# Softmax on one core: late loads as two tiles of 15 and 13 rows, first load on SyncE, first store held for the third tile

## Chip, cores, metric

One core of a Trainium2 chip. The metric is device time in microseconds (us), the median of several executions of the whole program; "span" is the profiled part of one execution, from its first instruction to its end, and the time is 1.8 us more than the span. All runs quoted here were fast, with a granted clock of 1.0. Ratios are the mean time of one kernel's fast runs over the mean of the other's fast runs of the same rounds, so they are not quite the ratio of the medians quoted beside them. ACT is ScalarE, DVE is VectorE, POOL is GpSimd; SyncE (SP) computes nothing here and issues transfers.

## The reference

```python
x = np.random.randn(16, 1024, 512).astype(np.float32)
x_scaled = x / 2.0
x_max = np.max(x_scaled, axis=-1, keepdims=True)
exp_x = np.exp(x_scaled - x_max)
return exp_x / np.sum(exp_x, axis=-1, keepdims=True)
```

A softmax over 512 columns. The 16384 rows lie as 128 rows on each of 128 partitions; "a row" below means one of these 128, that is 128 x 512 x 4 bytes = 262 KB. 33.55 MB come in and 33.55 MB go out.

## The kernel before

A plan lists the tiles: rows of each chunk, and the place in a buffer of 100 rows. The first eight tiles (3, 7 and six times 15 rows) fill the buffer. The last four go to places that become free; their loads are called late loads. A tile is one transfer; the numbers in its list are its chunks, the rows that DVE and ACT work on at a time.

```python
PLAN = [
    ([3], 0), ([4, 3], 3), ([5] * 3, 10), ([5] * 3, 25), ([5] * 3, 40), ([5] * 3, 55),
    ([5] * 3, 70), ([5] * 3, 85), ([5] * 3, 10), ([4, 3], 3), ([3], 0), ([3], 25),
]
LAG = 2
AFTER = {8: 4, 9: 4, 10: 4, 11: 6}     # late load 8 is issued after tile 4's exponentials, ...
...
# ACT: exponentials; late loads, each behind the stores that free its place
for k, (t, b, c, a) in enumerate(chunks):
    while late and last_chunk[AFTER[late[0]]] < k:
        u = late.pop(0)
        for v in behind[u]:
            nc.scalar.wait_ge(st[v], 16)
        nc.scalar.dma_start(out=sb(u), in_=dram(xf, u)).then_inc(ld[u], 16)
    ...                                # one activation (exp, with its sum) for each row
# DVE: maximum of chunk k, then 1/sum and product of chunk k - 2
for k in range(len(chunks) + LAG):
    if k < len(chunks):
        do_max(k)
    if k >= LAG:
        do_mul(k - LAG)
# SyncE: stores, in order of the tiles
for t in range(len(tiles)):
    nc.sync.wait_ge(s_mul, last_chunk[t] + 1)
    nc.sync.dma_start(out=dram(of, t), in_=sb(t)).then_inc(...)
```

All loads go out on ACT's queue (q10 in the profile), all stores on SyncE's (q1). Tiles are counted from 0, as in the code; the prediction says "the ninth tile" for tile 8.

## Time and profile before

| | before |
|---|---|
| time | 162.19 us (162.18 to 162.22, 4 runs) |
| span of the profiled run | 160.4 us |
| DVE, ACT busy | 132.0 us (82%), 94.5 us (59%) |
| moved | 67.1 MB, 419 GB/s over the span |
| last two loads land | 135.7 and 146.6 us |

The prediction shows the lines of the page, and reads from them that bytes set the time.

### The profile page before, as it was taken

The page shows a single profiled execution, that of the slowest core. Times are in us where ns is not written, and L with a number is a line of the kernel's source. Part 1 is how long each engine was busy: PE and PEld are TensorE (multiplying, and loading weights), DVE is VectorE, ACT ScalarE, POOL GpSimd, SP SyncE. Part 2 cuts the span into 40 slices and gives each one's busy share as a digit, 9 for nine tenths or more (in the row PEclk, how much of TensorE's full clock was granted, in tenths as well). Part 3 has the DMA queues.
Part 4 walks back from the last instruction along what each step waited for, and adds up shares of the span by engine and source line. Part 5 has one row for each costly group of instructions (what it writes and reads, how often), then busy time and mean ns, then how long its engine had stood idle before and what let it go on. Part 6 is the DMA issues. An engine that isn't in the chain of part 4 may idle for free.

```text
span 160.4 us, 480 instructions
## 1 busy us (share of the span) xinstructions
DVE 132.0 (82%) x155; ACT 94.5 (59%) x257; POOL 0.2 (0%) x4
## 2 busy tenths in 40 slices
DVE  0475499999999999999999999999999997704900
ACT  0739076759548646866679666697666875500500
POOL 0000000000000000000000000000000000000000
DMA  7999999999998999999999999998999999999796
GB/s 259 483 402 467 397 426 411 343 464 420 417 483 383 475 391 467 429 429 439 414 460 406 467 391 469 398 467 376 474 432 423 441 429 432 411 448 432 335 408 245
DMA packets 3459, 67.13 MB, mean 419 GB/s; under 512 B 384, under 2 KB 384, under 8 KB 1152
## 3 DMA queue, kind: packets, MB, share of 16 engines
q10 hardware_dynamic: 1728, 33.56, 49.5%
q1 hardware_dynamic: 1728, 33.56, 48.8%
q14 instruction: 3, 0.02, 0.0%
HBM read 33.55 MB, written 33.55 MB: 418 GB/s over the span
## 4 chain that ended last, share of the span: by engine, by line
DVE 49%; DMA 38%; another core or an unknown queue 5%; ACT 1%; issue 0%; DVEq 0%
DMA arena<-in_x_dram 38%; DVE negmax L91 25%; DVE arena L104 13%; DVE arena L111 10%; ACT arena L130 1%; DVE recip L100 1%; DVEq L206 0%
## 5 line engine op out<-in xcount | busy, mean ns | idle before, releaser
L130 ACT ACTIVATE arena<-arena,negmax 128x512 f32<-128x512 f32 x128 | 90.8, 710 | 51.6 <-DVE negmax L91 51.6
L91 DVE TENSOR_REDUCE negmax<-arena 128x5 f32<-128x2560 f32 (+2 forms) x28 | 72.3, 2586 | 19.6 <-DMA arena<-in_x_dram 19.5
L111 DVE TENSOR_SCALAR arena<-arena,recip 128x512 f32<-128x512 f32 x91 | 37.9, 482 | 0.7
L130 ACT ACTIVATION_READ_ACCUMULATOR arena<-arena,negmax 128x1 f32 x128 | 23.9, 187 | 0.0
L104 DVE TENSOR_TENSOR arena<-arena,recip 128x2560 f32<-128x2560 f32 (+2 forms) x8 | 21.0, 2625 | 0.3
L100 DVE RECIPROCAL recip<-sums 128x5 f32<-128x5 f32 (+2 forms) x28 | 4.9, 176 | 0.0
L130 ACT ACT_TABLE_LOAD x1 | 1.3, 1283 | 4.5 <-issue 4.5
L195 POOL MEMSET const-bfloat16-1.0<- 128x1 bf16 x1 | 0.1, 101 | 0.0
L195 POOL MEMSET const-uint8-127<- 128x1 uint8 x1 | 0.1, 101 | 0.0
L195 POOL MEMSET const-float32-0.0<- 128x1 f32 x1 | 0.1, 98 | 0.2 <-issue 0.2
L195 POOL MEMSET const-float32-1.0<- 128x1 f32 x1 | 0.1, 98 | 0.0
## 6 DMA issues: line engine op xcount, KB each, us to landing
arena<-in_x_dram ACTq DMA_DIRECT2D x7, 3840.0 KB, 44.9
out_dram<-arena SPq DMA_DIRECT2D x7, 3840.0 KB, 23.1
arena<-in_x_dram ACTq DMA_DIRECT2D x2, 1792.0 KB, 33.1
out_dram<-arena SPq DMA_DIRECT2D x2, 1792.0 KB, 11.7
arena<-in_x_dram ACTq DMA_DIRECT2D x3, 768.0 KB, 52.2
out_dram<-arena SPq DMA_DIRECT2D x3, 768.0 KB, 6.7
```

The source lines that it names most:

```text
L91: nc.vector.reduce_max(out=negmax[:, b : b + c], in_=arena[:, a : a + c], axis=mybir.AxisListType.X, negate=True,)._wait_ge(ld[t], 16).the ...
L100: nc.vector.reciprocal(out=recip[:, b : b + c], in_=sums[:, b : b + c])._wait_ge(s_exp, k + 1).then_inc(s_rec, 1)
L104: nc.vector.tensor_mul(out=arena[:, a : a + c], in0=arena[:, a : a + c], in1=recip[:, b : b + c].unsqueeze(2).to_broadcast([P, c, D]),)._w ...
L111: ins = nc.vector.tensor_scalar_mul(out=arena[:, a + r], in0=arena[:, a + r], scalar1=recip[:, b + r : b + r + 1],)
L130: ins = nc.scalar.activation(out=arena[:, a + r], in_=arena[:, a + r], func=mybir.ActivationFunctionType.Exp, bias=negmax[:, b + r : b + r ...
L195: nc = _bacc.Bacc("TRN2", target_bir_lowering=False, num_devices=1)
```

## The change

The intent: fewer and larger late transfers, whose packets hold their own against the stores' packets; the first load from an engine that is free; stores kept out of the way of the first loads. At the end, GpSimd's four waits for stores that landed long before are taken out.

```diff
-    ([5] * 3, 70), ([5] * 3, 85), ([5] * 3, 10), ([4, 3], 3), ([3], 0), ([3], 25),
+    ([5] * 3, 70), ([5] * 3, 85), ([5] * 3, 0), ([5, 4, 4], 15),
 ]
+HOLD = 2
-AFTER = {8: 4, 9: 4, 10: 4, 11: 6}
+AFTER = {8: 4, 9: 6}
@@ issue_loads
-            if t not in behind:
+            if t in behind:
+                continue
+            if t == 0:
+                nc.sync.dma_start(out=sb(t), in_=dram(xf, t)).then_inc(ld[t], 16)
+            else:
                 nc.scalar.dma_start(out=sb(t), in_=dram(xf, t)).then_inc(ld[t], 16)
@@ stores
-            nc.sync.wait_ge(s_mul, last_chunk[t] + 1)
+            nc.sync.wait_ge(s_mul, last_chunk[max(t, HOLD)] + 1)
@@ end
-        for t in awaited:
-            nc.gpsimd.wait_ge(st[t], 16)
         nc.gpsimd.wait_ge(s_end, 16 * (len(tiles) - len(awaited)))
```

## The prediction

> **What bounds the kernel now.** I read the page's slices and queues first, then the traffic by stretches, then DVE's and ACT's instructions in order of time, then single DMA issues with their time to landing.
>
> The slices say that the 16 DMA engines are busy from the second slice to the last but one:
>
> ```profile
> DMA  7999999999998999999999999998999999999796
> DMA packets 3459, 67.13 MB, mean 419 GB/s; under 512 B 384, under 2 KB 384, under 8 KB 1152
> ...
> DVE 132.0 (82%) x155; ACT 94.5 (59%) x257; POOL 0.2 (0%) x4
> ```
>
> No compute engine has more than 82%. The traffic by stretches (columns: stretch, its length, busy time of DVE, ACT, POOL, clock, DMA share, GB/s):
>
> ```profile
> 0.00:1.00 1.00, 0.00 (x0) 0.00 (x0) 0.20 (x4) 1.00 0.00 0
> 1.00:2.00 1.00, 0.00 (x0) 0.00 (x0) 0.00 (x0) 1.00 0.85 197
> ...
> 14.00:28.00 14.00, 10.16 (x8) 7.89 (x23) 0.00 (x0) 1.00 0.97 409
> ...
> 111.00:135.00 24.00, 23.27 (x36) 17.86 (x50) 0.00 (x0) 1.00 1.01 433
> 135.00:148.00 13.00, 4.87 (x7) 2.23 (x6) 0.00 (x0) 1.00 1.01 433
> 148.00:150.00 2.00, 1.93 (x7) 1.57 (x5) 0.00 (x0) 1.00 0.71 307
> 150.00:152.00 2.00, 1.97 (x6) 0.66 (x2) 0.00 (x0) 1.00 0.82 344
> ...
> 159.20:160.40 1.20, 0.00 (x0) 0.00 (x0) 0.00 (x0) 1.00 0.00 0
> ```
>
> The full rate is 433 GB/s, and it holds from 135 to 148 us although DVE works only 4.87 of those 13 us. So DVE's waits there cost nothing: bytes set the time. 67.1 MB at 433 GB/s take 155.0 us; the span is 160.4. The other 5.4 us are what a change can touch. From the same answers (length minus MB over 433): 0 to 4 us lose 1.6; 4 to 14 us seem to gain 0.4, because packets are booked by their start; 14 to 28 us lose 0.8; 28 to 148 us lose 0.2 together; 148 to 160.4 us (324 GB/s) lose 3.1. Of these 3.1, 1.0 lies in 148 to 152, 0.9 in 152 to 159.2, 1.2 after the last data.
>
> Why 148 to 152 runs short shows DVE's order:
>
> ```profile
> 137.57 1.68 DVE L111 TENSOR_SCALAR arena<-arena,recip 128x512 f32<-128x512 f32 x4
> 146.65 1.75 DVE L91 TENSOR_REDUCE negmax<-arena 128x3 f32<-128x1536 f32 x1 [7.40 <-DMA arena<-in_x_dram]
> 148.32 0.17 DVE L100 RECIPROCAL recip<-sums 128x3 f32<-128x3 f32 x1
> 148.52 1.28 DVE L111 TENSOR_SCALAR arena<-arena,recip 128x512 f32<-128x512 f32 x3
> ```
>
> The multiply of the tenth tile (148.52) stands in DVE's order behind the maximum of the twelfth, whose load landed at 146.6. Three stores (1.8, 0.8, 0.8 MB) come free only at 149.8 and later, when the ninth tile's store is just running out.
>
> **What the skill says.** "DMA: Bandwidth & Descriptors", section "Where 436 GB/s comes from", gives a ceiling of 435.2 GB/s for the 16 ports. The trace agrees: 433, for reads alone and for stores beside reads. So the change can't raise the rate. The same page, "Queues, rings and completion order": an engine goes round-robin between queues, packet by packet. The trace agrees, with a row of 3 x 2 KB against one of 15 x 2 KB (loads q10, stores q1, from 18 to 27 us: packets, MB):
>
> ```profile
> q10 hardware_dynamic: 109, 3.35, 86.8%
> q1 hardware_dynamic: 109, 0.67, 17.7%
> ```
>
> Equal packets, a fifth of the bytes. From 135 to 140 us it is the other way: 60 load packets have 0.36 MB against 1.60 MB in 52 store packets. So the 3-row late loads were starved by 15-row stores, and took 68.2 and 52.2 us to land. And the page's section "Issuing engines are not separate DMA queues" says that another issuing engine saves issue time alone; the trace of before can't show it.
>
> **The change part by part.**
>
> *First load on SyncE.* ACT's eight issues take 335 to 623 ns each, from 0.13 to 4.4 us. The 7-row load can now be issued about 0.6 us earlier, and both queues feed the engines from 1.3 us on. Of the 1.6 us lost before 4 us I give it 0.2; the first 1.3 us are latency. The two loads now share by packets (6 KB and 14 KB), so the first tile lands after some 20 x 128 KB = 2.6 MB, at about 7.4 us in place of 4.65. That is hidden: DVE stands idle for 3.77 us before the third tile at 18.08 anyway.
>
> *First store waits.* Stores 0, 1 and 2 are all issued when the third tile is multiplied, 44.97 now, 44.7 after (0.3 earlier from the head). Loads run alone until then: 100 rows x 262 KB = 26.2 MB are asked for at the start, and 433 GB/s x 43 us is 18.6 MB, so the engines don't run dry. It saves one change from loads alone to loads beside stores (lost: part of the 0.8 in 14 to 28, and a little after 30 us). I give it 0.2 us.
>
> *Where this comes back.* The ninth tile's load waits on ACT for stores 0, 1 and 2, ahead of the exponentials of chunk 12. Now the third store lands at 44.97 + 21.5 = 66.5, which is just when that load goes out (66.52); chunk 12's maximum ends at 69.7, so ACT loses nothing. After, the three stores (25 rows, 6.55 MB) start at 44.7 behind nothing but share with loads; the loads in queue run out first (12 packets per engine left, against 24 of the stores). So the third store lands when 26.2 + 6.55 = 32.8 MB have moved: 1.3 + 32.8/0.433 + 1 us lost = 78 us, 78.5 with the semaphore. ACT is held there until 78.5 + 0.4 (one DMA issue), its five exponentials take 3.6 us (69.71 to 73.3 in the trace), so chunk 12's sums are ready at 82.6. DVE wants them at 79.2. So ACT stands still for about 9 us and DVE for 3.3; DVE's clock runs 3.0 us late from there on. At 82.6 the backlog of stores is a full tile, so the DMA engines don't notice.
>
> *Late loads.* The ninth tile's load goes out at 79 in place of 66.5, and shares 1:1 with stores: it lands near 99 (wanted at 114.3). The last one, 13 rows, waits for store 3 (near 93) and for ACT's place in the order (97.5): it shares 26 KB against 30 KB packets, lands near 118, wanted at 129.3. Before, the last lands were 135.7 and 146.6. So DVE's waits of 1.11 and 7.40 us vanish, and so does the dry stretch at 148 to 152.
>
> *The end.* DVE at the fifth-last step begins at 126.33 + 3.0 = 129.3. Then: maximum 5 rows, multiply 5 rows, 4.9; maximum 4 rows 2.2 + multiply 5 rows 2.2 = 4.4 (store of the ninth tile at 138.7); another 4.4 to 143.1; two multiplies of 4 rows with reciprocals, 1.8 each: 146.7. DMA at 138.7 has moved (138.7 - 2.4) x 0.433 = 59.0 MB, of it 33.6 loads, so 25.5 stores of 26.2 available: 0.7 MB or 1.7 us of stores in hand. At 146.7, 28.9 of 30.1: 2.8 us in hand. A new store needs about 1 us to its first data. So the engines stay fed, but barely at 138.7.
>
> *Small parts.* Four waits of GpSimd on semaphores long reached: nothing. One chunk less on DVE: some 0.2 us, hidden. Two stores of 6 KB rows less at the end (421 and 369 GB/s there): 0.2.
>
> *Sum.* Lost after: head 1.2 - 0.2 = 1.0; middle 1.0 - 0.2 = 0.8; tail 3.1 - 1.0 (dry stretch) - 0.2 = 1.9. Span 155.0 + 3.7 = 158.7; time is span + 1.8 (162.19 against 160.4): 160.5. To this I add 0.6: the engines' completion is ragged by up to 2 us in loads at 109 to 111 (the trace's packet records), the dry stretch now realigns them and would no longer do so, and 138.7 is close. Prediction 161.1.
>
> **Rivals.** *Tail starved by ACT's stop.* If the third store lands 2 us later than 78, DVE is 2 us later still, and 1.7 us of stores in hand are gone: a gap of 1 to 2 us and 162 to 163. For it: the thin margin. Against: the landing follows from bytes alone. *All overhead but latency goes.* 1.3 to the first data, 155.0, 1.3 at the end and 1.8 outside: 159.4 at the least; even that is 1.7% faster. For it: pure streams run at 433. Against: starts and changes of stream always showed some loss. *Nothing gained.* Stores held until 44 us are only moved, and the tail is 155 us of bytes: 162.2. Against: the trace's dry stretch has a cause that the plan removes. *A load too late.* If the ninth tile landed after 114, DVE would wait; 15 us of room speak against it.
>
> **Range and chances.** Bytes set a floor of 159.4, so faster by over 2% (below 158.9) is all but out. Slower by over 2% (above 165.4) needs a gap over 4 us that I can't find. Range 160.1 to 162.4.
>
> **What would show it.** Right: queue q1 carries only the first load until 45 us; ACT idle some 9 us before 79 and DVE 3 us near 80; the ninth load issued near 79, the last landing before 120; no DVE wait for a load after 20 us; 148 to 156 us at 430 GB/s. Wrong: DMA share under 0.9 in any stretch of 2 us between 130 and 150, DVE waiting for a load after 100 us, or a lower rate while loads run alone.

## The result, and the profile after

The changed kernel takes 161.95 us (161.65 to 162.22, 4 runs) against 162.19: ratio 0.9984, 95% interval 0.9966 to 1.0002. On another chip, in five rounds, it was 0.9989 (0.9977 to 1.0001). The measured time is inside the range, but of the 1.1 us that I forecast only about 0.2 came, and neither interval excludes that nothing came.

First the page of the changed kernel, then all its waits (who waited, for whom: us in total, times, longest):

```profile
span 159.9 us, 474 instructions
...
DVE 131.5 (82%) x153; ACT 93.9 (59%) x257; POOL 0.2 (0%) x4
...
DMA  7999898999999999999999999999999898999993
```

```profile
ACT arena L137 <- DVE negmax L98: 46.3, 21, 11.5
DVE negmax L98 <- DMA arena<-in_x_dram: 10.7, 2, 7.0
ACT L137 <- issue: 4.2, 1, 4.2
DVE recip L107 <- ACT arena L137: 4.0, 1, 4.0
POOL const-float32-0.0 L200 <- issue: 0.2, 1, 0.2
```

DVE waits for a load only twice, both before 18 us (7.0 and 3.7); its waits of 1.11 and 7.40 us for the late loads are gone. In their place stands one wait of 4.0 us for ACT. Instructions of the changed kernel in order of time, around it (start, length, what, and the idle time before in brackets), with one piece of the chain of work that ended last (start, length, what) in front:

```profile
45.52 33.56 DMA out_dram<-arena
```

```profile
79.19 0.33 ACTq L135 DMA_DIRECT2D arena<-in_x_dram  x1
79.57 0.72 ACT L137 ACTIVATE arena<-arena,negmax 128x512 f32<-128x512 f32 x1 [11.49 <-DVE negmax L98]
```

```profile
83.24 0.19 DVE L107 RECIPROCAL recip<-sums 128x5 f32<-128x5 f32 x1 [4.04 <-ACT arena L137]
```

ACT stood still for 11.49 us. The page puts that down to DVE's maximum, but that was ready long before (at about 69.3 us); what ended last was the landing of store 2 at 79.1, in front of ACT's load. Counted from 69.3 the stop is some 10 us, where I had about 9. So the predicted stop is there, at the predicted place: 79 us, and 4.0 us on DVE where I had 3.3.

The traffic of the changed kernel at the end (stretch, length, busy time of DVE, ACT, POOL, clock, DMA share, GB/s):

```profile
148.00:156.00 8.00, 0.00 (x0) 0.00 (x0) 0.00 (x0) 1.00 1.01 436
156.00:157.00 1.00, 0.00 (x0) 0.00 (x0) 0.00 (x0) 1.00 0.99 426
157.00:158.00 1.00, 0.00 (x0) 0.00 (x0) 0.00 (x0) 1.00 0.25 107
```

The dry stretch of before (307 and 344 GB/s between 148 and 152 us) is gone, as predicted. And yet the end did not come 1 us sooner. Why shows in the last slices, where each DMA engine begins its last packet. Here are 40 slices of 0.04 us of the changed kernel from 156.4 to 158.0 us; a packet of 26 KB is booked where it starts and shows as some 666 GB/s, so 1331 is two engines:

```profile
GB/s 1331 0 666 1331 1331 0 666 1331 1331 1331 1331 0 0 0 0 0 0 0 0 0 0 0 0 0 666 0 0 0 1331 666 0 0 0 0 0 0 0 0 0 0
```

From 156.4 to 156.84 there are 16 starts, twelve of them an engine's last; the other four engines begin theirs at 157.36 to 157.56. The trace also holds a record of every packet (queue, start, length, size), which no view prints one by one; "packet records" below means these, read by a script. "Lost" time is the time since the first data less the bytes moved over the full rate, so it counts idle engines and slow packets alike, as a mean over the 16 engines. By the packet records, the 16 engines end between 157.42 and 158.54 us: twelve together and four up to 1.1 us late; the twelve take over nothing of what the four still have to do. In the kernel before it looked different. The same view of before, from 150.4 to 152.0 us, where the store of tile 9 begins after the dry stretch (a 14 KB packet shows as some 358):

```profile
GB/s 0 0 0 0 0 0 2150 1434 1075 717 358 0 0 0 0 0 0 0 0 358 2150 1792 717 717 0 0 0 0 0 0 0 0 358 2150 1075 1434 358 358 0 0
```

All 16 engines begin within 0.2 us of one another. They had ended the store before between 149.83 and 150.79 us. So in the dry stretch the fast engines waited up to 0.97 us, and four hardly at all.

Counted from the first data, the mean of the 16 ends is 156.87 us in the changed kernel against 157.69 before, but the last end is 157.54 against 157.79. The mean engine ends 0.82 us sooner, the last one only 0.25 us. (Each is one profiled run.)

That is the theory which the experiments test. **Theory S**: each of the 16 DMA engines has its own sixteenth of every transfer (8 packets of 128) and can't help another; the time is set by the slowest few of the 16; the dry stretch was slack of the fast ones, and taking it away only moves their waiting to the end. **Rival M**: the missing bytes of the dry stretch cost what they say, 1.0 us, and another part of the change ate the gain.

### The profile page after: what moved, and what is told of

Same layout as the page of the kernel before. It is cut to its first block, busy times and chain, and to the rows that moved or that the text cites. A ratio compares the mean times of both kernels' runs of the same rounds, so it can differ in the third digit from the quotient of the medians.

```text
span 159.9 us, 474 instructions
## 1 busy us (share of the span) xinstructions
DVE 131.5 (82%) x153; ACT 93.9 (59%) x257; POOL 0.2 (0%) x4
## 4 chain that ended last, share of the span: by engine, by line
DVE 56%; DMA 32%; ACT 2%; issue 0%; SPq 0%; DVEq 0%; ACTq 0%
DVE negmax L98 28%; DMA out_dram<-arena 21%; DVE arena L118 19%; DMA arena<-in_x_dram 11%; DVE arena L111 8%; ACT arena L137 2%; DVE recip L107 1%; SPq L159 0%; DVEq L211 0%; ACTq L135 0%; ACTq L134 0%
```

## The experiments

Each kernel ran beside the kernel before on the same chip (five rounds). The kernel before took 162.17, 162.36 and 162.23 us.

**Dry stretch alone taken away.** The kernel before, with DVE's order changed at one point.

```diff
-            if k >= LAG:
+            if k >= LAG and k - LAG != last_chunk[9]:
                 do_mul(k - LAG)
+            if k == last_chunk[10]:
+                do_mul(last_chunk[9])
```

> The kernel before, with one thing changed: DVE multiplies the tenth tile before it takes the maximum of the twelfth, so that a store of 1.8 MB is in the queue at about 141 us and the DMA queue no longer runs dry at 150 us. Theory S (a few slow engines set the end, the dry stretch was slack of the faster ones): 162.0 to 162.3, no gain over 0.2 us; the fast engines now end 0.6 to 0.9 us ahead of the slow ones in the last store. Rival M (the dry stretch cost what its missing bytes say, as predicted): 1.0 us less, 161.2.

Measured: 162.36 us against 162.17, ratio 1.0008 (0.9994 to 1.0021). No gain. The store of tile 9 was in the queue at 140.6 us, and by the packet records no engine was idle between 146 and 153 us. The stretches of this kernel:

```profile
149.00:150.00 1.00, 0.77 (x2) 1.00 (x5) 0.00 (x0) 1.00 0.77 328
150.00:151.00 1.00, 0.30 (x2) 0.63 (x2) 0.00 (x0) 1.00 0.84 358
...
157.00:158.00 1.00, 0.00 (x0) 0.00 (x0) 0.00 (x0) 1.00 0.81 338
```

Two things follow. The 16 engines now end between 156.48 and 157.60 us after the first data, 1.1 us apart; before, it was 157.62 to 157.79. The fast ones gained 1.1 us and the last one 0.2 (the profiled run, 161.95 us, was the fastest of six, so even this 0.2 is no gain of the kernel). And the view still shows 328 and 358 GB/s at 149 to 151 us with engines that are never idle: packets are booked where they start, and the change from 30 KB to 14 KB packets looks like a hole. From 148 to 152 us this view shows a mean of 383 GB/s, which by the prediction's arithmetic "lost" 4 x (1 - 383/433) = 0.46 us. So of the 1.0 us that I read from the same view of before, about half was the way it books packets; the rest was 0.55 us of mean idle time, on engines that were early.

**Late loads alone.** The kernel before with the new plan and order of late loads, nothing else.

```diff
-    ([5] * 3, 70), ([5] * 3, 85), ([5] * 3, 10), ([4, 3], 3), ([3], 0), ([3], 25),
+    ([5] * 3, 70), ([5] * 3, 85), ([5] * 3, 0), ([5, 4, 4], 15),
-AFTER = {8: 4, 9: 4, 10: 4, 11: 6}
+AFTER = {8: 4, 9: 6}
```

> The kernel before with only the late loads changed (two tiles of 15 and 13 rows); first load on ACT, no hold. Theory S: 161.8 to 162.2, because the dry stretch that it removes was slack and only the two small stores less at the end count (0.1 to 0.2 us). Rival M: 161.0 to 161.3. ACT's stop near 79 us should be gone or short, as store 2 then lands near 66 us.

Measured: 161.95 against 162.17, ratio 0.9990 (0.9977 to 1.0002): 0.16 us (interval -0.03 to 0.37), as theory S has it; rival M's 1.0 is outside. One source of such a gain is in the packet records: after 153 us the 6 KB packets of the last stores lose 0.2 us in the kernel before and nothing here, where the last stores have larger packets. ACT's stop is not there (its longest wait is 4.6 us).

**Dry stretch put back.**

```diff
+            if k == len(chunks) + LAG - 1:
+                nc.vector.reduce_max(
+                    out=junk[:, 0:5], in_=arena[:, 85:90], axis=mybir.AxisListType.X
+                )
             if k >= LAG:
                 do_mul(k - LAG)
```

> The changed kernel with a dry stretch put back on purpose: one more 5-row maximum (2.8 us, into an unused buffer) ahead of DVE's last multiply, so the last store goes out at about 149.9 us in place of 147.1, when the store before ends between 149.8 and 150.9 us on the 16 engines. Theory S: fast engines wait up to 0.9 us, slow ones hardly, and the time moves by 0.0 to 0.25 us. Rival M: it is longer by about the bytes missed, 0.6 to 1.0 us.

Measured: 162.21, ratio 1.0007 to the kernel before (0.9995 to 1.0019). Against the changed kernel's 0.9984 and 0.9989 on other chips that is 0.3 to 0.4 us more: above theory S's 0.25, below M's 0.6. The stretches show the hole:

```profile
149.00:150.00 1.00, 1.00 (x3) 0.00 (x0) 0.00 (x0) 1.00 0.36 154
150.00:151.00 1.00, 0.15 (x1) 0.00 (x0) 0.00 (x0) 1.00 0.00 0
151.00:152.00 1.00, 0.00 (x0) 0.00 (x0) 0.00 (x0) 1.00 1.12 479
```

The last store went out at 150.1, and its data began at 151.0 us, when the slowest engine had ended at about 150.9. The hole by the packet records is 1.1 us in the mean (1.56 us lost at 149 us, 2.64 at 153), and the time grew by a third of that. The engines then end 0.15 us apart. By these ends the slowest engine waited only some 0.1 us, so theory S as it stands doesn't explain the 0.3 to 0.4 us; across chips and with these intervals they may be noise. Open.

**Hold until the fourth tile.** `HOLD = 3` in the changed kernel.

> The changed kernel with the first store held for the fourth tile (about 61.7 us), when the loads of the first 100 rows are nearly done (62 us at 433 GB/s). If what makes engines slow is the start of stores underneath a full load queue (0.4 to 0.6 us of lost time near 47 to 53 us in the trace after), that loss goes and the time falls by 0.2 to 0.8 us, to 161.2 to 161.7, with the engines' ends closer together. If it is something else, the time stays within 0.2 us. ACT's stop should be about as long (store 2 still lands near 78 us).

Measured: 162.87, ratio 1.0041 (1.0028 to 1.0054): slower by 0.7 us than before, so this idea failed. The first loads had all but ended (near 62 us) when the first store data came at 62.7 us, which still cost 0.5 us between 60 and 66 us, about as much as the start beneath loads in the changed kernel (0.6 us between 44 and 60 us); and then the start of load 8 beneath stores cost more:

```profile
80.00:86.00 6.00, 2.30 (x7) 6.00 (x17) 0.00 (x0) 1.00 1.05 384
...
92.00:100.00 8.00, 7.93 (x13) 7.15 (x22) 0.00 (x0) 1.00 0.97 388
```

By the packet records 1.5 us are lost between 80 and 100 us: 30 KB store packets that take 1.14 us elsewhere take up to 2.28 us at 84 us.

**No hold.** `HOLD = 0` in the changed kernel; run twice, on two chips.

> The changed kernel without the hold: stores go out as each tile is ready. ACT's stop at 69 to 79 us goes (store 2 lands near 66 us), DVE's 4 us wait with it. Since DMA is the bound, the time should stay within 0.3 us of the changed kernel's 161.95. If the hold was worth the 0.2 us that I predicted, it is 162.1 to 162.2; if the stop on ACT had cost time, it is below 161.5.

> The changed kernel without the hold, again. If the 0.4% by which it beat the kernel before on another chip is the hold's cost, it is 0.3 to 0.6 us below the changed kernel here. If that was the chip or the draw of slow engines, the two are within 0.15 us.

Measured: 161.54 against 162.36, ratio 0.9956 (0.9935 to 0.9978), and 161.78 against 162.23, ratio 0.9967 (0.9954 to 0.9980). The changed kernel itself on the second of these chips:

> The changed kernel once more, to stand beside the next two on the same chip. 161.6 to 162.3, 0.0 to 0.4 us below the kernel before.

Measured: 162.01, ratio 0.9989. So the hold costs 0.0022 of the time, about 0.36 us (0.23 by the medians; the two intervals overlap by 0.0003), and dropping it makes the fastest version. DVE's delay is hidden as it was predicted to be: by the packet records of the changed kernel no engine stands idle after it. In the mean the 16 engines end at 156.87 and 156.90 us after the first data with the hold and at 156.69 and 156.70 without, 0.2 us sooner. The packet records show where the hold loses time. In all five profiles with the hold for the third tile (changed kernel, the runs with the gap, with ACT's first load, with small late tiles, and the repeat) 0.26 to 0.35 us are lost between 90 and 100 us; in both profiles without hold, nothing is lost there. Load packets at 92 us take up to 1.76 us in the changed kernel. The hold also makes ACT stop, and the stop sends load 8 out at 79.19 us in place of 67.00; these runs don't separate the two. With `HOLD = 1` (below) ACT stops too, for 7.55 us, and load 8 goes out at 75.21, but nothing is lost between 90 and 100 us: a stop alone need not cost.

**First load back on ACT.**

```diff
             if t == 0:
-                nc.sync.dma_start(out=sb(t), in_=dram(xf, t)).then_inc(ld[t], 16)
+                nc.scalar.dma_start(out=sb(t), in_=dram(xf, t)).then_inc(ld[t], 16)
```

> The changed kernel with the first load back on ACT. The prediction gave 0.2 us to SyncE's issue; the lost time in the first 8 us was the same in both traces (0.75 and 0.73 us), so I expect no change: within 0.15 us of 161.95, and the first maximum at 4.7 us in place of 7.0.

Measured: 162.24 against 162.36, ratio 0.9992 (0.9971 to 1.0013). In time, not told apart from the changed kernel's 0.9984. In the traces there is one steady difference: data starts 1.01 us after the span's start where SyncE issues the first load (0.99 to 1.02 in nine profiles) and 1.14 to 1.17 where ACT does (five), because ACT's first instruction comes at 0.12 to 0.13 us and SyncE's at 0.00. That is worth 0.13 us; the rest of the start is the same.

**Late loads back in four tiles, with the other parts kept.**

```diff
-    ([5] * 3, 70), ([5] * 3, 85), ([5] * 3, 0), ([5, 4, 4], 15),
+    ([5] * 3, 70), ([5] * 3, 85), ([5] * 3, 10), ([4, 3], 3), ([3], 0), ([3], 25),
-AFTER = {8: 4, 9: 6}
+AFTER = {8: 4, 9: 4, 10: 4, 11: 6}
```

> The changed kernel with the late loads back in four small tiles. By theory S about 162.0 to 162.3 (a dry stretch again at the end, as slack of the fast engines). By rival M 1.0 us above the changed kernel, 162.9.

Measured: 162.58 against 162.36, ratio 1.0010 (0.9991 to 1.0029). 0.0026 above the changed kernel's ratio, 0.4 us: more than the 0.16 us of the late loads alone, less than half of M's 1.0. Its dry stretch (0.5 us of mean idle time) lies before 146 us.

**The transfers alone.** No work on DVE and ACT, each store waits for its load. Its output is wrong, which doesn't matter for the time.

```diff
-            nc.sync.wait_ge(s_mul, last_chunk[max(t, HOLD)] + 1)
+            nc.sync.wait_ge(ld[t], 16)
```

> Wrong result on purpose: the transfers of the changed kernel alone, each store waiting only for its load, with no work on DVE and ACT. It shows the floor of these bytes on these queues. If only the slowest engine's stream counts in the real kernels, this is 161.0 to 162.0 and there is next to nothing to gain; if waits of DVE or ACT still cost something, it is below 160.8. Lower bound from bytes: 159.4.

Measured: 162.93 us (161.57 to 163.91), ratio 1.0039 (1.0000 to 1.0079). The bare transfers are not faster than the softmax. I had expected 161 to 162; in the profiled run their 16 engines end at 157.57 us in the mean, 0.7 us later than in the changed kernel, and farthest apart, 2.35 us. Their stores start earlier; that this is the cause is not shown. A kernel without any wait for DVE or ACT is thus not faster, so nothing here speaks for a cost of those waits; but it is no floor either, since its transfers meet in another order.

**Hold until the second tile.** `HOLD = 1` in the changed kernel.

> The changed kernel with the first store held only for the second tile (about 27.6 us), so that stores 0 and 1 start together and the store queue starts up once beneath the loads, not twice. If each start-up of a second stream makes some engines slow (0.25 us mean near 18 us and 0.5 us near 31 us without hold, 0.4 to 0.6 near 48 us with it), one of the two goes and this is 0.1 to 0.3 us below the version without hold. If start-ups don't add up on the same engines, it is equal to it within 0.15 us.

Measured: 161.89, ratio 0.9977 (0.9963 to 0.9991), 0.1 us above the version without hold: equal within the noise. One start of stores less did not help.

**GpSimd's four waits alone.** The kernel before without them.

```diff
-        for t in awaited:
-            nc.gpsimd.wait_ge(st[t], 16)
```

> The kernel before without GpSimd's four waits on stores that landed long ago. From the last data to the end of the span the traces have 1.39 to 1.42 us with these waits (three kernels) and 1.31 to 1.33 us in six of seven kernels without. If the waits cause that, 0.1 us comes off (162.1 against 162.2), and the profile shows 1.3 us after the last data; the prediction said nothing. If another part of the change does, 1.4 us stays.

Measured: 162.21 against 162.23, ratio 1.0000 (0.9989 to 1.0012). The profile shows 1.32 us after the last data, as expected; in time the 0.1 us can't be seen. Not settled, and small.

**Where the 16 engines end**, from the packet records, in us after the first data, in all profiles whose end has no dry stretch:

| kernel | time of this run | first engine ends | last engine ends |
|---|---|---|---|
| no hold | 161.54 | 156.30 | 157.43 |
| changed | 161.65 | 156.41 | 157.54 |
| late loads alone | 161.85 | 156.45 | 157.54 |
| before, DVE's order changed | 161.95 | 156.48 | 157.60 |
| hold until second tile | 162.00 | 156.34 | 157.89 |
| no hold, second chip | 162.03 | 156.35 | 157.92 |
| first load on ACT | 162.22 | 156.43 | 157.98 |
| changed, again | 162.28 | 156.52 | 158.17 |
| hold until fourth tile | 162.93 | 157.87 | 158.69 |
| transfers alone | 162.97 | 156.52 | 158.87 |

But for the one kernel that lost 1.5 us on all engines, the first engine always ends at 156.3 to 156.5 us, whatever the kernel, and in eight of the ten the mean of the 16 ends is 156.7 to 156.9. That the time follows the last engine, to within 0.25 us, is no finding by itself, since the span ends 1.3 to 1.4 us after the last data. The finding is that only the last end moves, by 0.7 us over these eight, down to the differences between two runs of one kernel: 0.5 us without hold, 0.6 us in the changed kernel.

## Why the prediction was right or wrong

*The bound*, 433 GB/s and bytes, was right, and so were the schedule's steps: ACT's stop at 79 us, DVE's wait (4.0 against 3.3 us), the load of tile 8 at 79.19 us, no late wait for a load, DVE's last multiply (done at 147.2 against 146.7), and engines that stay fed. The rivals of a starved tail and of a load too late did not come.

*The step that failed* is in the sum: "tail 3.1 - 1.0 (dry stretch) - 0.2". It took the bytes missing from a mean rate for time of the kernel. Taken away by itself, the dry stretch gave no gain: the kernel was 0.13 us slower (1.0008; the interval is 0.10 us faster to 0.34 slower). About half of the term was the view's booking of packets by their start; the other half was idle time of engines that were early. What counts is the last of 16 engines, and in the dry stretch the latest ones hardly waited: the whole change brought the mean engine home 0.82 us sooner and the last one 0.25. I had seen the second point and set 0.6 us against the sum for it, but took the rest for real. So the late loads were forecast at 1.0 + 0.2 - 0.6 = 0.6 us and brought 0.16. The 0.2 in it for the small stores fits the packet records (0.2 us).

*Hold, a gain of 0.2 us*: it has the wrong sign, and as a miss it is as large as the first (0.56 against 0.44 us). It costs about 0.36 us (0.9989 against 0.9967 on one chip). The start of stores beneath loads at 14 to 34 us was saved, as I said; but it came again at 44 to 60 us, and load packets grew slow once more at 92 us, which I did not foresee.

*Head, 0.2 us*: the traces show 0.13, in time unresolved. The 7-row load was issued 0.42 us earlier (0.12 against 0.54), not 0.6.

*GpSimd's waits, nothing*: in time, nothing.

*The sign of being wrong*, a DMA share under 0.9 in 2 us between 130 and 150, was a bad one: the view shows 0.85 at 134 to 136 and 0.82 at 142 to 144 us in the changed kernel, while by the packet records no engine was idle there. It is the same booking again.

The parts don't add up cleanly. Without hold the gain is 0.53 and 0.71 us (0.9967 and 0.9956). Of this 0.16 is the late loads', so 0.37 to 0.55 is left over for SyncE's first load and GpSimd's waits, and tested by themselves these gave 0.05 to 0.13 and 0.0 us. The remainder is not explained; each of these figures has an interval of about 0.2 us or more to either side.

*Open*: why packets grow slow for some microseconds where one queue's transfers start beneath the other's, and why a few engines (four in most profiles) lose more than the others. The trace does not name a packet's engine, so I can't say whether they are always the same.

## What to carry to other kernels

Where the DMA engines are the bound, don't price a hole in the mean GB/s: look at where each engine ends its share of a transfer. The hole of 0.55 us in the mean cost nothing here, since the engines that stood idle were early, and the test was cheap: one reordered piece of DVE's work took the hole away and gained nothing. Holding stores back to keep the first loads clear only moved the meeting of the two streams to a later moment: no better with `HOLD = 1`, and worse with 2 and 3.

## What the Trainium skill lacked or had wrong

- "DMA: Bandwidth & Descriptors", section "Queues, rings and completion order", has the round-robin by packets, which the trace shows, but nothing on what happens where a second queue's transfers start beneath the first's: 30 KB packets that take 1.14 us take up to 1.85 us near 30 us in the kernel before, and up to 2.28 us at 84 us with the hold until the fourth tile; each such start lost 0.2 to 1.5 us in the mean of the engines.
- The same page says in "Why a DMA increments its semaphore by 16 and not by 1" that the engines finish independently, but gives no size: in the last store they ended 0.15 to 2.35 us apart, and among eight kernels whose mean end was 156.7 to 156.9 us after the first data, the last end went from 157.43 to 158.17.
- The same page's table "Specifications" has about 0.6 us to the first byte on this path, and doesn't say from where it counts. With empty queues the first data came 1.01 us after the start of SyncE's first issue, but 0.63 us after its end (the issue takes 0.38 us), so the figure fits from the issue's end. It says nothing of full queues: a store beneath a full load queue had its first data after 3.9 to 4.2 us (14.33 to 18.19 before, 44.65 to 48.80 after).
- No page says that traffic by time slices counts a packet where it starts: a change from 30 KB to 14 KB packets looked like 0.46 us of idle time in engines that were never idle.
